# Encoder block on one core: row maxima a step earlier, a sixth score buffer, the next bias after its group, and another bank for one of the first conv units

## The chip, the cores and the metric

The kernel runs on one core of a Trainium2 chip, as one program with one launch. The metric is device time in microseconds (us) of one execution, first instruction to last; lower is better. Of the kernel before there are three timed runs and one profiled execution. The engines are called by the names that the profile uses: PE (matmuls), PEld (its weight loads), DVE (vector), ACT (activation), POOL (GpSimd), SP (which here only issues DMAs).

## The reference, cut to what matters

```python
D_MODEL = 1024; SEQ = 1024; GRID_W = 64; N_HEADS = 8; HEAD_DIM = 64

def reference(x, ...):
    u = rms_norm(x, norm1_g)
    q, k, v, cb, cc, ch, ga, gb = split(u @ w_in)
    q = rms_norm(q per head, q_norm_g); k = rms_norm(k per head, k_norm_g)
    y_a = neighbourhood_attention(q, k, v, rpb) @ w_attn_branch
    y_b = short_gated_conv(cb, cc, ch, conv_w) @ w_conv_branch
    x = x + (sigmoid(ga) * y_a + sigmoid(gb) * y_b) @ w_o
    h = rms_norm(x, norm2_g) @ w_mlp_in
    return x + square(relu(h)) @ w_mlp_out

def neighbourhood_attention(q, k, v, rpb):
    s = q k^T / sqrt(64) + bias            # 8 x 16 window on the 16 x 64 grid
    s = where(mask, s, -1e30)
    return softmax(s) @ v

def short_gated_conv(cb, cc, ch, w):       # depthwise, width 3
    z = pad(cc * ch)
    return cb * (z[:-2] * w[0] + z[1:-1] * w[1] + z[2:] * w[2])
```

Everything is float32 outside. Inside, each matmul operand is split into a high and a low half of 16 bits, and a product takes three passes (high by high, high by low, low by high).

## The kernel before

The program goes through stages on one core: the norm of x and the projections to q, k and v; a stage in which **attention and the gated conv run together**; the gates and branch products; w_o; the MLP. The change lies in the second of these, 157 to about 345 us after the span's start.

In that stage one loop (L1127) counts steps k from 0 to N + 12, with N = 64. A step stands for one *score*: head pair p = k // 16, block i of 128 queries, head e of the pair. Only the order of the instructions within the loop sets the order on each engine; every engine takes its own instructions strictly in the order in which the loop emits them, and waits on semaphores where another engine's result or buffer isn't ready.

- **Scores.** At every fourth step `at_qk(k)` (L949) emits the matmuls (L954) of four scores, k to k+3, into four score banks of PSUM, `sbank`: three with the tag "s" and one with the tag "o" (L945). A bank can be written again when the row maximum of its old score has read it.
- **Row maxima.** `at_max(s)` (L958) reads the bank on DVE, adds the bias, writes the sum to an SBUF buffer `sz` (`z`, five buffers) and leaves the row's extreme in a column of `sc`. In the trace this is the pair CUSTOM_DVE_ANT_0 and DVE_READ_ACCUMULATOR2_ANT; in the lists of instruction order it is "ISA sz,sc" and "ISA sc". Step k emits the maximum of score k-1. So the fourth maximum of a group is emitted at the step in which the next group's matmuls are emitted, just ahead of them.
- **The rest of a score.** `at_exp` on ACT (step k+1), `at_recip` on DVE, `at_hi` on ACT (the high half of P), `at_lo` on DVE (the low half, "P<-sz,sc,P"), `at_turn` (a transposing DMA from P to PT on SP's queue), `at_pv` (matmuls L1030, twelve steps after the scores) and `at_out` (qD, the attention's result, first on ACT, then on DVE).
- **The bias of the next head pair.** `bias_load` at step 3 of 16, and `bias_make` (L507: one DVE operation, "bias<-bias,sc,mk", and one on POOL, "biasm") for the two heads at steps 9 and 11.
- **Conv and gate matmuls** (L1049) fill PE between the score groups: `emit(n)` takes the next n from a generator, 9 a step at first, then 8, 6, 7, 4. A unit of 24 goes to one of three banks with the tag "d". Its reader is `conv_post` (L829): an ACT copy (L837) for the first of three kinds, DVE multiplications ("z<-ps_d,z", "cv<-ps_d,cv") for the others.
- **Weights of the next conv chunk** are split by ACT and DVE ("w_ws<-raw,sc"). `tick` moves this preparation on; `deal` gives each step up to four ticks, by a reckoning of how much DVE and ACT work was emitted in the step. At a chunk's boundary `flush` emits what is left.

The first two conv units are emitted ahead of the loop (L809), into two banks with the tag "o". There are two such banks, given out in turn, and the next two users of the tag are the fourth score bank and `hbank`, where `at_pv` writes. The copies L837 of these two units go to the conv's buffer `z`, which lies in memory that the q/k stage used until its last transposing DMA (kD<-k, L546) landed; `sz` lies there too.

Near the stage's end the scale of a gate weight (chunk S1) is worked out by `scale_s1`: its second raw tile is loaded by SP, ACT scales and squares it, DVE writes a column of `ones`, and PE sums that column over the partitions (L221, "ps_d<-ones"). `scale_of(am, more, n)` holds this matmul back until PE has been given n times 6144 more columns of work.

Of the kernel before, what the change touches and what calls it, by code (L numbers as in the profile page):

```python
# [10 lines left out]
F32 = mybir.dt.float32  # L11
# [82 lines left out]
def encoder_block(ctx: ExitStack, tc: tile.TileContext, x, weights, cols, gqk, rel, masks, out):  # L94
# [13 lines left out]
    def bank(tag):  # L108
        return psum.tile([128, 512], F32, name="ps_" + tag, tag=tag, bufs=banks[tag])
# [6 lines left out]
    def anybank():  # L116
        rc[0] += 1
        return bank("d" if solo[0] else "dsodsods"[rc[0] % 8])
# [6 lines left out]
    def cols_of(kind, n):  # L125
        a = area[kind]
        if a[1] + n > a[2]:
            assert kind != "keep"
            a[1] = a[0]
        a[1] += n  # L130
        return slice(a[1] - n, a[1])

    def keep(n=1):
        return cols_of("keep", n)

    def tmp(n=1):
        return cols_of("tmp", n)
# [64 lines left out]
    def apart(mark, n=3, of=units):  # L202
        while of[0] < mark + n and not forced[0]:
            yield WAIT
# [15 lines left out]
    def all_sum(a, out, bk, floor, lag=1):  # L220
        T.matmul(bk[:, 0:1], ones[:, 0:128], a, start=True, stop=True)  # L221
        yield
        yield from apart(units[0], lag)
        V.tensor_scalar(sc[:, out], bk[:, 0:1], floor, None, op0=OP.max)
        yield
# [145 lines left out]
    def push(*chunks):  # L371
        for ch in chunks:
            bg.append(ch.prep())
# [6 lines left out]
    for (kind, j), pieces in plan():  # L380
        ch = chunks[kind, j] = Chunk(kind, [(nk, sum(n for _, n in cs)) for _, _, nk, cs in pieces],
                                     {"A": "wa", "B": "wb"}.get(kind, "ws"), rows.get(kind, lambda j: g1)(j),
                                     j if kind == "V" else None, 9 if kind in "VQKCGS" else 0)
# [77 lines left out]
    def pow2_half(ss, top, s, inv, more=0):  # L461

        V.tensor_scalar(sci[:, ss], sci[:, ss], EXP, None, op0=OP.bitwise_and)
        yield
        V.tensor_scalar(sci[:, ss], sci[:, ss], 1.0, float(1 << 23), op0=OP.mult, op1=OP.add)
        yield
        V.tensor_scalar(sci[:, ss], sci[:, ss], 1, EXP, op0=OP.logical_shift_right, op1=OP.bitwise_and)
        yield
        V.tensor_scalar(sci[:, s], sci[:, ss], -1.0, float((190 + top) << 23), op0=OP.mult, op1=OP.add)  # L469
        V.tensor_scalar(sci[:, inv], sci[:, ss], 1.0, float((64 - top - more) << 23), op0=OP.mult, op1=OP.add)  # L470
        yield
# [30 lines left out]
    def bias_load(p):  # L502
        t = wbias.tile([128, 2, 3, 128], F32, name="bias")
        SP.dma_start(t.rearrange("p e b k -> p (e b k)"), rel[p])
        m = wbias.tile([128, 2, 384], F32, name="biasm")
        return t, m

    def bias_make(t, m, e):
        te = t[:, e].rearrange("p b k -> p (b k)")
        V.scalar_tensor_tensor(te, te, sc[:, cinv], mk[:, 0], op0=OP.mult, op1=OP.add)  # L510
        G.tensor_tensor(m[:, e], te, mk[:, 1], op=OP.add)
# [252 lines left out]
    for n, (kind, b) in enumerate(todo):  # L764
        ch = cQ if kind == "q" else cK
        if kind == "k" and b == 0:
            push(cConv[0])
        if n == 4:
# [14 lines left out]
            bias = {0: bias_load(0)}  # L783
# [22 lines left out]

    conv_start(0)
    push(cConv[1])
    first = [bank("o"), bank("o")]  # L809
    for half in range(2):  # L810
        unit(ch_mms(first[half], actU, half, cConv[0], 8, 384, 0), None, 8, 4)
        finish_qk(13 + half)
# [9 lines left out]
    w2p = p2.enter_context(tc.tile_pool(name="p2", bufs=2))  # L822
# [112 lines left out]
    N = len(steps)  # L935
    st = {}

    def rng(i):
        lo, hi = max(i - 1, 0), min(i + 1, 7)
        return lo, hi - lo + 1  # L940
# [18 lines left out]
    def at_max(s):  # L959
        p, i, e = steps[s]  # L960
        d = st[s]
        t, m = bias[p]
        if 0 < i < 7:
            bm = m[:, e]
        else:
            bm = (t[:, e, 1:3] if i == 0 else t[:, e, 0:2]).rearrange("p b k -> p (b k)")
        z = d["z"] = w2p.tile([128, 384], F32, name="sz", bufs=5)
        d["mx"] = tmp()
        V.tensor_tensor_reduce(z[:, :d["n"]], d["ps"][:, :d["n"]], bm, sc[:, cneg], 3.0e38, OP.add, OP.min,
                               accum_out=sc[:, d["mx"]])  # L970
# [36 lines left out]
    def at_pv(s):  # L1007
        p, i, _ = steps[s]
        O, PT = hbank, st[s]["PT"]
        (lo0, nb0), (lo1, nb1) = rng(i), rng(i + 1)  # L1010

        def place(u, e, sp, kb):
            lo, nb = ((lo0, nb0), (lo1, nb1))[u]
            return 12 * u + (2 * e + sp) * nb + kb - lo

        seq = [(kb, sp, sv) for kb in (i, i + 1, i - 1, i + 2) if 0 <= kb < 8 for sp, sv in PASSES]
        for n, (kb, sp, sv) in enumerate(seq):
            us = [u for u in range(2) if (lo0, lo1)[u] <= kb < ((lo0, lo1)[u] + (nb0, nb1)[u])]
            for e in range(2):
                hd = (2 * p + e) * HD  # L1020
                a = place(us[0], e, sp, kb)
                c = (i % 4 + us[0]) * 128
                if len(us) == 2:
                    b = place(1, e, sp, kb)
                    r = PT[:, a:b + 1:b - a]
                    o = O[64 * e:64 * e + 64, c:c + 256]
                else:
                    r = PT[:, a]
                    o = O[64 * e:64 * e + 64, c:c + 128]
                T.matmul(o, VT[:, kb, sv, hd:hd + HD], r, start=n == 0, stop=n == len(seq) - 1)  # L1030
        for e in range(4):
            del st[s + e]
# [25 lines left out]
    def sum_of(sm):  # L1058

        b, a = cols_of("prep", 1), ones_col()  # L1060
        V.tensor_reduce(sc[:, b], sc[:, sm], axis=AX, op=OP.add)
        V.tensor_copy(a, sc[:, b])
        return a, work[0]

    def scale_of(am, more, n=3):

        a, mark = am
        yield from apart(mark, n * 6144, work)
        b, s, inv = cols_of("prep", 1), cols_of("prep", 1), keep()
        yield from all_sum(a, b, anybank(), 1e-36)  # L1070
        yield from pow2_half(b, 14, s, inv, more)
        return s, inv

    def rows_scaled(ch, g):

        for i in range(2):
            while len(ch.raw) <= i:
                yield WAIT
            for k in range(4):
                v = ch.raw[i].rearrange("p (n k c) -> p k n c", n=2, k=4)[:, k]  # L1080
                A.activation(v, v, AF.Copy, scale=sc[:, at(g, 4 * i + k)])  # L1081
            yield

    def squares(ch, junk):

        sm = cols_of("prep", 2)
        for i in range(2):
            while len(ch.raw) <= i:
                yield WAIT
            A.activation(junk, ch.raw[i], AF.Square, accum_out=sc[:, at(sm, i)])  # L1090
            yield
        return sm

    def scale_s1():

        ch = cS[1]
        yield from rows_scaled(ch, g1)
        while len(conv_done) < 4:
            yield WAIT
        z = w2p.tile([128, S + 2], F32, name="z", bufs=1).bitcast(BF16)[:, :1024]  # L1100
        sm = yield from squares(ch, z)
        am = sum_of(sm)
        yield
        ch.s, ch.inv = yield from scale_of(am, 9, 1)

    meters = V, A = Meter(nc.vector, 0.96, 150), Meter(nc.scalar, 1.2, 190)
    debt, mark = [0.0, 0.0], [0.0, 0.0]
# [1 line left out]
    def share(k):  # L1109
        return 9 if k < 6 else 8 if k < 55 else 6 if k < 64 else 7 if k < 73 else 4  # L1110
# [16 lines left out]
    for k in range(N + 13):  # L1127
        p, w = k // 16, k % 16
        if p < 3 and w == 3:
            bias[p + 1] = bias_load(p + 1)  # L1130
        if p < 3 and w in (9, 11):
            bias_make(*bias[p + 1], (w - 9) // 2)
        ok = lambda d: 0 <= k - d < N
        early = min(4 if k % 4 else 5, share(k))
        emit(early)
        if ok(1):
            at_max(k - 1)
        if k % 4 == 0:
            if ok(0):
                at_qk(k)  # L1140
            if ok(12):
                at_pv(k - 12)
        if ok(4):
            at_hi(k - 4)
        if k % 2 and ok(3):
            at_recip(k - 3)
        if ok(5):
            at_lo(k - 5)
        if k % 2 == 0 and ok(6):
            at_turn(k - 6)  # L1150
        if ok(1):
            at_exp(k - 1)
        if 35 <= k < 59 and k % 3 == 2:
            turn_piece(1, 0, (k - 35) // 3)
        if 66 <= k < 74:
            turn_piece(2, 2, k - 66)
        if k == 60:
            bg.append(scale_s1())
        units[0] += 1
        conv_step(0)  # L1160
        if k % 4 == 2 and ok(14):
            at_out(k - 14, 0)
        if k % 4 == 3 and ok(15):
            at_out(k - 15, 1)
        deal(k)
        account(k)
        emit(share(k) - early)
# [744 lines left out]
    for n in range(28):  # L1912
        s, o = n // 7, n % 7
# [92 lines left out]
```

## Time and profile before

| what | us |
|---|---|
| timed runs: lowest, median, highest | 1224.27, 1225.31, 1226.7 |
| the profiled execution | 1225.52 |
| its span, first to last instruction | 1223.4 |
| PE busy in the span | 1192.3 (97%) |
| DVE, ACT, POOL busy | 932.5, 754.3, 450.1 |
| stage of the change, 157 to 345: PE, DVE, ACT busy of 188 | 176.84, 141.00, 130.62 |

PE's matmuls overlap each other in the list of instructions by time (a 128x512 matmul is shown with 379 ns, and its successor begins about 216 ns later), so PE's losses are read from idle time, not from durations. In square brackets such a list gives the idle time just before an instruction and what ended it. The granted clock is a share of PE's full speed.

### The profile page before, as it was taken

What the parts mean: (1) busy time and instruction counts of PE and PEld (TensorE: products, weight loads), DVE (VectorE), ACT (ScalarE), POOL (GpSimd) and SP (SyncE); (2) the same over time, 40 slices, a digit from 0 to 9 for tenths busy, and PEclk for the clock granted to TensorE, in tenths of its full rate; (3) what the DMA queues carried; (4) which work ended last, traced back from release to release, by engine and by line L of the source; (5) the groups of instructions that cost most, each with busy time, mean ns of one, the idle gap of its engine ahead of it and who ended that gap; (6) DMA issues with size and microseconds to landing.
All of it is one profiled execution on the core that took longest, in us unless ns stands there. A gap on an engine that the chain in (4) does not pass through costs nothing.

```text
span 1223.4 us, 16820 instructions
## 1 busy us (share of the span) xinstructions
PE 1192.3 (97%) x6166; PEld 570.4 (47%) x6166; DVE 932.5 (76%) x1743; ACT 754.3 (62%) x1178; POOL 450.1 (37%) x300
## 2 busy tenths in 40 slices
PE   6999999999999999999999999999999999999998
PEld 5444434444444444444458444444444444444444
DVE  7877767888668686887887665555448999998997
ACT  6756657777654454535768887787776754646440
POOL 5720012231321111101003665755647572563562
PEclk9999999999999999999999999999999999999999
DMA  7746435667551211216096654454484935335202
GB/s 256 178 165 126 104 80 111 126 118 154 113 155 37 68 56 48 69 35 259 18 179 148 207 189 143 142 189 150 135 292 163 345 128 193 152 129 199 103 35 103
DMA packets 162674, 171.24 MB, mean 140 GB/s; under 512 B 123296, under 2 KB 123808, under 8 KB 158496
## 3 DMA queue, kind: packets, MB, share of 16 engines
q1 hardware_dynamic: 162592, 170.17, 47.0%
q8 instruction: 48, 0.79, 0.3%
q14 instruction: 34, 0.28, 0.1%
HBM read 102.51 MB, written 37.75 MB: 115 GB/s over the span
## 4 chain that ended last, share of the span: by engine, by line
PE 79%; DVE 11%; ACT 3%; issue 3%; DMA 2%; POOL 1%; SPq 0%; DVEq 0%; ACTq 0%; POOLq 0%
PE ps_d L230 27%; PE ps_s L230 24%; PE ps_o L230 20%; PE ps_d L1049 4%; DVE P L89 1%; DVE sz L89 1%; PE ps_d L708 1%; DVE w_ws L89 1%; DVE sc L89 1%; DMA u2T<-v 1%; PE ps_s L708 1%; DMA raw<-in_weights 1%; ACT w_ws L89 1%; PE ps_o L1030 1%; DVE w_s L1215 1%
## 5 line engine op out<-in xcount | busy, mean ns | idle before, releaser
L230 PEld LDWEIGHTS <-ops 128*128 128x128 f16 x1356 | 132.4, 98 | 157.3
L230 PEld LDWEIGHTS <-w 128*128 128x128 f16 x1368 | 132.8, 98 | 140.7 <-DMA u2T<-v 1.3
L1049 PE MATMUL ps_d<-uT,w_ws 128*128 128x512 f16 x576 | 131.2, 386 | 0.0
L230 PE MATMUL ps_s<-ops 128*128 128x512 f16 (+1 forms) x528 | 118.3, 374 | 0.0
L230 PE MATMUL ps_d<-ops 128*128 128x512 f16 x504 | 115.6, 379 | 0.0
L230 PE MATMUL ps_d<-u2T,w 128*128 128x512 f16 (+1 forms) x504 | 110.1, 371 | 0.0
L1826 ACT ACTIVATE ops<-hf,sc 128x2048 f16<-128x2048 f32 x26 | 52.0, 1998 | 91.7 <-PE ps_d L230 54.1
L1202 POOL TENSOR_TENSOR tsum<-raw 128x512 f32<-128x512 f32 x28 | 47.3, 1703 | 141.6 <-ACT raw L1081 141.6
L1406 POOL TENSOR_TENSOR as<-as 128x512 f32<-128x512 f32 x60 | 82.5, 1376 | 41.6 <-ACT as L1686 38.0
L230 PEld LDWEIGHTS <-w_s 128*128 128x128 f16 x588 | 56.8, 98 | 69.0 <-DVE w_s L1215 0.9
L1049 PEld LDWEIGHTS <-w_ws 128*128 128x128 f16 x576 | 55.3, 99 | 67.6 <-issue 4.8
L230 PE MATMUL ps_s<-u2x,w 128*128 128x512 f16 (+1 forms) x348 | 78.6, 375 | 0.0
L1828 DVE SCALAR_TENSOR_TENSOR ops<-hf,sc,ops 128x2048 f16<-128x2048 f32 x26 | 73.0, 2808 | 4.0 <-ACT ops L1826 2.9
L1081 ACT ACTIVATE raw<-raw,sc 128x256 f32<-128x256 f32 x164 | 67.6, 494 | 11.5 <-DMA raw<-in_weights 11.5
L230 PE MATMUL ps_o<-ops 128*128 128x512 f16 x324 | 74.3, 379 | 0.0
L1202 POOL TENSOR_TENSOR gsum<-raw 128x512 f32<-128x512 f32 x14 | 18.6, 1350 | 127.1 <-ACT raw L1081 73.4
L1219 ACT ACTIVATE w<-raw,sc 128x512 f16<-128x512 f32 (+1 forms) x28 | 24.7, 928 | 52.2 <-DVE sc L469 52.2
L89 ACT ACTIVATE sz<-sz,sc 128x384 f32<-128x384 f32 (+1 forms) x64 | 37.2, 582 | 29.9 <-DVE sc L89 29.6
L1719 DVE TENSOR_TENSOR as<-ps_s,as 128x512 f32<-128x512 f32 x13 | 9.0, 692 | 57.9 <-ACT as L1738 57.9
L1842 POOL TENSOR_TENSOR raw<-raw 128x1024 f32<-128x1024 f32 x8 | 30.8, 3864 | 36.8 <-DVE ops L1836 36.8
L230 PE MATMUL ps_o<-u2T,w 128*128 128x512 f16 (+1 forms) x204 | 44.2, 366 | 0.0
L230 PEld LDWEIGHTS <-uT 128*128 128x128 f16 x288 | 28.1, 98 | 33.7
(384 smaller groups left out, 2629.8 us busy)
## 6 DMA issues: line engine op xcount, KB each, us to landing
raw<-in_weights SPq DMA_DIRECT2D x89, 512.0 KB, 5.5
hs<-as SPq DMA_DIRECT2D x16, 1792.0 KB, 8.7
hf<-hs SPq DMA_DIRECT2D x26, 1024.0 KB, 6.6
w2x<-in_weights SPq DMA_DIRECT2D x16, 512.0 KB, 7.5
raw<-in_weights SPq DMA_DIRECT2D x16, 384.0 KB, 3.6
xt<-in_x SPq DMA_DIRECT2D x8, 512.0 KB, 10.0
gs<-s SPq DMA_DIRECT2D x4, 1024.0 KB, 4.8
x<-in_x SPq DMA_DIRECT2D x8, 512.0 KB, 9.8
```

The lines of the kernel that those rows point to most:

```text
L89: return f(out, *a, **kw)
L230: T.matmul(ps, l, r, start=a, stop=b)
L708: T.matmul(vbank["q", b], UT[:, sa, k, b * 128:(b + 1) * 128], cQ.parts[:, sw, 512 * k:512 * k + 512], start=(k, n) == (0, 0), stop=(k, n) ...
L1030: T.matmul(o, VT[:, kb, sv, hd:hd + HD], r, start=n == 0, stop=n == len(seq) - 1)
L1049: T.matmul(ps, l, r, start=a, stop=b)
L1081: A.activation(v, v, AF.Copy, scale=sc[:, at(g, 4 * i + k)])
L1202: G.tensor_tensor(t[:, o], a, b, op=OP.add)
L1219: A.activation(o(0), w, AF.Copy, scale=sc[:, s])
L1406: sub.tensor_tensor(z[o], z[a], z[b], op=op)
L1826: A.activation(P[:, 1, 0], hf, AF.Copy, scale=sc[:, Rs])
L1828: V.scalar_tensor_tensor(P[:, 1, 1], hf, sc[:, Rs], P[:, 1, 0], op0=OP.mult, op1=OP.subtract)
L1842: G.tensor_tensor(w11[i2], w11[i2], w12[i2], op=OP.add)
```

## The change

Five edits, all in the attention and conv stage:

1. the second of the two first conv units goes to a "d" bank instead of an "o" bank;
2. `sz` has six buffers instead of five;
3. of a group of four scores, the first maximum stays at the step after the matmuls; the second and third come together at the next step, and the fourth a step later. The third and fourth, and with them the group's last, are thus one step sooner, and none is left at the step that emits the next group's matmuls;
4. the second `bias_make` is at step 12 of 16 instead of 11, which puts it behind the group's last maximum;
5. the factor of the S1 scale's delay is 1.4 instead of 1.

```diff
-    first = [bank("o"), bank("o")]
+    first = [bank("o"), bank("d")]
...
-        z = d["z"] = w2p.tile([128, 384], F32, name="sz", bufs=5)
+        z = d["z"] = w2p.tile([128, 384], F32, name="sz", bufs=6)
...
-        ch.s, ch.inv = yield from scale_of(am, 9, 1)
+        ch.s, ch.inv = yield from scale_of(am, 9, 1.4)
...
-        if p < 3 and w in (9, 11):
-            bias_make(*bias[p + 1], (w - 9) // 2)
         ok = lambda d: 0 <= k - d < N
         early = min(4 if k % 4 else 5, share(k))
         emit(early)
-        if ok(1):
-            at_max(k - 1)
+        for s in ((k - 1,), (k - 1, k), (k,), ())[(k - 1) % 4]:
+            if 0 <= s < N:
+                at_max(s)
         if k % 4 == 0:
             if ok(0):
                 at_qk(k)
             if ok(12):
                 at_pv(k - 12)
+        if p < 3 and w in (9, 12):
+            bias_make(*bias[p + 1], w // 12)
```

How rows move on three queues. First **ACT, at the start of the stage**, before (-) and now (+); the two L837 rows are the copies of the two first conv units:

```order
 L820 ACT_TABLE_LOAD
 L820 ACTIVATE sc<-sc 128x1
-L837 ACTIVATE z<-ps_o,sc 128x4x16x8 x2
+L837 ACTIVATE z<-ps_o,sc 128x4x16x8
+L837 ACTIVATE z<-ps_d,sc 128x4x16x8
```

The second copy now reads a "d" bank, and the fourth score bank falls on the "o" bank whose last reader was an ACT copy of the k projection, twelve ACT rows earlier.

Second, **DVE around the last maximum of scores 24 to 27** (the row "sz,sc<-ps_o"), for which the matmuls of scores 28 to 31 wait. Before:

```order
L89 SCALAR_TENSOR_TENSOR w_ws<-raw,sc,w_ws 128x384
L89 SCALAR_TENSOR_TENSOR bias<-bias,sc,mk 128x384
L89 ISA sz,sc<-ps_s,biasm,sc 128x384
L89 ISA sc 128x1
L89 RECIPROCAL sc<-sc 128x2
L89 TENSOR_SCALAR sc<-sc 128x2
L89 SCALAR_TENSOR_TENSOR P_2248<-sz,sc,P_2248 128x384
L89 SCALAR_TENSOR_TENSOR qD<-ps_o,qD 128x512
L89 SCALAR_TENSOR_TENSOR w_ws<-raw,sc,w_ws 128x384
L89 ISA sz,sc<-ps_o,biasm,sc 128x384
L89 ISA sc 128x1
```

With the change:

```order
L89 ISA sz,sc<-ps_s,biasm,sc 128x384
L89 ISA sc 128x1
L89 SCALAR_TENSOR_TENSOR P_2204<-sz,sc,P_2204 128x384
L89 SCALAR_TENSOR_TENSOR w_ws<-raw,sc,w_ws 128x384
L89 ISA sz,sc<-ps_o,biasm,sc 128x384
L89 ISA sc 128x1
L89 RECIPROCAL sc<-sc 128x2
L89 TENSOR_SCALAR sc<-sc 128x2
L89 SCALAR_TENSOR_TENSOR P_2245<-sz,sc,P_2245 128x384
L89 SCALAR_TENSOR_TENSOR qD<-ps_o,qD 128x512
L89 SCALAR_TENSOR_TENSOR bias<-bias,sc,mk 128x384
```

The last maximum has moved ahead of the reciprocal pair, of one P row and of the qD row; the bias row, which stood ahead of it, stands behind it.

Third, **SP at the end of the attention**, where the second raw tile of S1 is loaded (L253). Before:

```order
L1005 DMA_TRANSPOSE PT<-P_3258 128x12x128
L1005 DMA_TRANSPOSE PT<-P_3319 128x12x128
L1056 DMA_TRANSPOSE qD<-gs 128x4x128
L253 DMA raw<-in_weights 128x1024
L1056 DMA_TRANSPOSE qD<-gs 128x4x128
```

With the change:

```order
L1005 DMA_TRANSPOSE PT<-P_3260 128x12x128
L253 DMA raw<-in_weights 128x1024
L1005 DMA_TRANSPOSE PT<-P_3319 128x12x128
L1056 DMA_TRANSPOSE qD<-gs 128x4x128 x2
```

The load now stands ahead of one PT transpose and one qD transpose that it used to follow. On PE the sum of S1's column (L221) stands seven conv matmuls earlier than before; no other PE row changes its place, and no operation is added or removed.

## The prediction

> **What bounds the kernel now.** I read the page's busy line first, then PE's list of waits for the stage, then the list by time around each wait.
>
> ```profile
> PE 1192.3 (97%) x6166; PEld 570.4 (47%) x6166; DVE 932.5 (76%) x1743; ACT 754.3 (62%) x1178; POOL 450.1 (37%) x300
> 157.00:345.00 188.00, 176.84 (x1168) 84.35 (x1166) 141.00 (x422) 130.62 (x304) 44.21 (x58) 0.98 0.57 118
> 345.00:1223.00 878.00, 873.12 (x4251) 412.95 (x4249) 669.79 (x1015) 519.80 (x686) 355.84 (x196) 1.00 0.43 141
> PE ps_o L954 <- DVE sc L89: 7.3, 6, 2.4
> PE ps_o L954 <- ACT z L837: 2.4, 1, 2.4
> ```
>
> PE is busy 97% of the span, so a microsecond is only to be had where PE stands still or runs slowly. The two rows of windows (length, then busy PE, PEld, DVE, ACT, POOL, clock) show where: 11.16 us of idle PE in the 188 us of attention and conv, 4.88 in the 878 us after. The waits, listed one by one, are the score matmuls that wait for a bank:
>
> ```profile
> 161.09 0.32 PE L954 MATMUL ps_o<-kD,qD 64*128 64x384 f16 x1 [2.39 <-ACT z L837]
> 180.85 0.32 PE L954 MATMUL ps_o<-kD,qD 64*128 64x384 f16 x1 [0.26 <-DVE sc L89]
> 189.63 0.27 PE L954 MATMUL ps_s<-kD,qD 64*128 64x256 f16 x1 [0.53 <-DVE sc L89]
> 191.64 0.27 PE L954 MATMUL ps_o<-kD,qD 64*128 64x256 f16 x1 [1.74 <-DVE sc L89]
> 232.20 0.27 PE L954 MATMUL ps_o<-kD,qD 64*128 64x256 f16 x1 [2.43 <-DVE sc L89]
> 270.70 0.27 PE L954 MATMUL ps_o<-kD,qD 64*128 64x256 f16 x1 [1.58 <-DVE sc L89]
> 280.16 0.32 PE L954 MATMUL ps_o<-kD,qD 64*128 64x384 f16 x1 [0.42 <-DVE sc L89]
> 290.53 0.32 PE L954 MATMUL ps_o<-kD,qD 64*128 64x384 f16 x1 [0.85 <-DVE sc L89]
> 329.66 0.18 PE L221 MATMUL ps_d<-ones 128*128 128x1 bf16 x1 [0.82 <-DVE sc L89]
> ```
>
> Those put down to DVE sum to 0.26 + 0.53 + 1.74 + 2.43 + 1.58 + 0.42 + 0.85 = 7.81 us, and nearly all are for the "o" bank, a group's fourth maximum. The idle time is not all that they cost. The windows of 3.4 us behind three of them (the clock is the number before the last two):
>
> ```profile
> 162.00:165.40 3.40, 3.40 (x12) 1.24 (x10) 0.56 (x5) 0.61 (x4) 0.00 (x0) 0.55 0.00 0
> 192.60:196.10 3.50, 3.50 (x20) 1.48 (x17) 2.20 (x9) 3.50 (x11) 0.00 (x0) 0.56 0.61 116
> 232.40:235.80 3.40, 3.40 (x34) 1.92 (x31) 3.15 (x10) 2.47 (x6) 0.00 (x0) 1.00 0.67 121
> ```
>
> After the waits of 2.39 and of 0.53 + 1.74 the clock falls to about half for one stretch of that length; after the 2.43 it doesn't. Each half-speed stretch loses 3.4 x 0.5 = 1.7 us.
>
> **The change part by part.** *The bank of a first conv unit.* What releases the 2.39 us is the copy of the first conv unit out of an "o" bank:
>
> ```profile
> 158.05 0.66 PE L954 MATMUL ps_s<-kD,qD 64*128 64x256 f16 x7
> 321.68 6.22 PE L1049 MATMUL ps_d<-uT,w_ws 128*128 128x512 f16 x28
> 160.29 1.37 ACT L837 ACTIVATE z<-ps_o,sc 128x512 f32<-128x512 f32 x2 [2.55 <-DMA kD<-k]
> 160.39 0.48 DVE L89 CUSTOM_DVE_ANT_0 sz<-ps_s,bias,sc 128x256 f32<-128x256 f32 x1 [3.20 <-DMA kD<-k]
> ```
>
> The copies can't begin before the last kD transpose has landed at 160.3, and that stays. But the fourth score bank now falls on the other "o" bank, whose reader was done long before; so the wait goes, and with it the slow stretch: -2.39 - 1.7 = **-4.1**. The price: the unit in a "d" bank is read until 160.29 + 1.37 = 161.66, and the third user of the "d" banks comes after the 24 matmuls of one unit and the sum's bank, at about 163.5 when PE doesn't stop (5 of the 24 are done when the scores begin at 158.05; these are 12 matmuls, 7 of which take 0.66, so some 1.2; 19 more at 6.22 / 28 = 0.22 take 4.2). The bank is free 1.8 us ahead of that; without this cover the edit would cost what is lacking. DVE can't begin earlier than 160.39, so PE is 4.1 us further ahead of it from here on.
>
> *Maxima sooner, bias behind.* No operation is added. I work out the wait of 2.43 from DVE's rows ahead of it:
>
> ```profile
> 227.12 0.99 DVE L89 SCALAR_TENSOR_TENSOR bias<-bias,sc,mk 128x384 f32<-128x384 f32 x1
> 228.57 0.15 DVE L89 RECIPROCAL sc<-sc 128x2 f32<-128x2 f32 x1
> 228.76 0.47 DVE L89 TENSOR_SCALAR sc<-sc 128x2 f32<-128x2 f32 x1
> 229.14 1.34 DVE L89 SCALAR_TENSOR_TENSOR P<-sz,sc,P 128x384 f16<-128x384 f32 x1
> 230.41 0.68 DVE L89 SCALAR_TENSOR_TENSOR qD<-ps_o,qD 128x512 f16<-128x512 f32 x1
> 231.53 0.61 DVE L89 CUSTOM_DVE_ANT_0 sz<-ps_o,biasm,sc 128x384 f32<-128x384 f32 x1
> ```
>
> By the order of rows, the bias (0.99) and all from the reciprocal to the maximum (231.53 - 228.57 = 2.96: reciprocal, scale, P, qD and one weight split) come to stand behind it. So it ends 3.9 us sooner, at about 228.3 instead of 232.15; PE wants the bank at 232.20 - 2.43 = 229.77. The wait goes with 1.5 to spare. In the same way the waits of 1.58, 0.42, 0.85 and 0.26 each have one step's DVE rows taken from ahead of them, more than they last. For the pair 0.53 + 1.74 it is closer, as PE comes 4.1 sooner there. DVE's windows between the score groups up to it, and its longest stop:
>
> ```profile
> 161.10:171.25 10.15, 10.15 (x43) 4.10 (x43) 4.29 (x18) 4.41 (x13) 0.00 (x0) 0.83 0.01 2
> 171.25:179.77 8.52, 8.52 (x47) 3.75 (x47) 7.02 (x19) 7.05 (x17) 0.00 (x0) 1.00 0.56 150
> 179.77:188.44 8.67, 8.41 (x45) 3.56 (x45) 8.63 (x17) 4.52 (x11) 5.22 (x6) 1.00 0.30 66
> 164.73 0.16 DVE L89 TENSOR_SCALAR sc<-ps_d 128x1 f32<-128x1 f32 x1 [3.44 <-PE ps_d L221]
> ```
>
> DVE is idle 5.86 + 1.50 + 0.04 = 7.4 us, 3.44 of it behind a sum on PE that came after the stall and the slow stretch. The rows that leave the front of the maximum (a bias, P, reciprocal and scale row, and a conv row) are about 2.2. The maximum ended just ahead of 191.64; less 2.2, and less some 5 of the idle time, it ends at about 184.4, and PE wants it at 191.64 - 1.74 - 0.53 - 0.26 - 4.1 = 185.0. I take a wait of 0.4 to be safe, too short to halve the clock (-1.7).
>
> *Where the stall goes.* DVE has the same work, so the next group is late where it is tight:
>
> ```profile
> 219.97:229.01 9.04, 9.04 (x64) 4.41 (x64) 8.76 (x18) 6.48 (x16) 5.08 (x6) 1.00 0.71 123
> 229.01:240.58 11.57, 9.14 (x65) 4.42 (x64) 9.70 (x26) 7.66 (x19) 1.13 (x4) 1.00 0.63 149
> 240.58:250.11 9.53, 9.38 (x70) 4.60 (x70) 7.31 (x29) 9.53 (x28) 1.12 (x1) 1.00 0.60 99
> 268.35:279.08 10.73, 9.15 (x65) 4.41 (x64) 10.52 (x26) 6.58 (x16) 4.39 (x7) 1.00 0.56 114
> 239.91 0.17 DVE L89 RECIPROCAL sc<-sc 128x2 f32<-128x2 f32 x1 [1.38 <-ACT sz L89]
> 240.84 0.48 DVE L89 CUSTOM_DVE_ANT_0 sz<-ps_o,bias,sc 128x256 f32<-128x256 f32 x1
> ```
>
> A group takes PE some 9.1 us; DVE's share between two groups is 8.76 + 9.70 = 18.46 in the pair up to 240.58, and 10.52 in the one from 268.35. Scores 32 to 35 start at 240.58, with PE wanting the fourth bank 0.66 later. Without the 2.43 it wants it at 238.8. DVE's last maximum started 240.84 - 231.53 = 9.3 us after that of the group before, of which 1.38 was idle; behind the earlier maximum there now stand 2.96 + 0.99 = 3.9 more and one weight split more (0.6), and a reciprocal, scale and P row less (1.0). That gives 9.3 - 1.4 + 3.9 + 0.6 - 1.0 = 11.4, and 228.3 + 11.4 = 239.7: about **+0.9** comes back. By the same count scores 48 to 51 get back about 1.0, for the row of 10.52 lies 1.4 over PE's pace and a chunk's weight splits end there. Bounds for all that comes back: nothing, if ACT's results come sooner too, and 4 us, if the two tight groups lose what their predecessors gain (2.43 + 1.58). I take 2.3 with the 0.4 above, nearer the middle, since the following groups have slack (7.31 of 9.53).
>
> *Sixth buffer, S1's delay.* A score's buffer is in use a step longer; with five, the third maximum of a group would wait for a P row. The sixth costs nothing that the trace shows. The S1 sum stands seven matmuls earlier on PE (1.5 us), and it waited 0.82 already; its load stands ahead of two transposes:
>
> ```profile
> 319.56 1.56 SPq L1056 DMA_TRANSPOSE qD<-gs  x1
> 321.16 0.59 SPq L253 DMA_DIRECT2D raw<-in_weights  x1
> 325.30 1.70 ACT L89 ACTIVATE raw<-raw,sc 128x256 f32<-128x256 f32 x4 [3.29 <-DMA raw<-in_weights]
> ```
>
> Two issues of about 1.5 make 3; 0.82 + 1.5 - 3 is below nothing, so the 0.82 goes or stays in part; bounds 0 and 2.3, taken 0.6.
>
> **Sum**, against the profiled 1225.52 (span 1223.4, and 2.1 around it): 2.39 + 1.7 + 7.81 + 1.7 + 0.82 = 14.4 at the most; 2.3 + 0.6 come back; -11.5 gives 1214.0. The profiled execution lies 0.2 over the median of the runs, 1225.31, and I let that go: **1214**.
>
> [...]
>
> **The rivals.** *DVE's late start holds PE at scores 12 to 15* (a wait in the place of the removed one). If none of DVE's 7.4 us of idle time goes, the maximum ends at 191.6 - 2.2 = 189.4, PE waits from 185.0, 4.4 us, and the clock halves again. The gain is 4.1 from the bank, 7.81 - 2.27 = 5.5 from the other waits, less 4.4 - 2.27 = 2.1 that the wait grows, less 2.3 that comes back elsewhere: 5.2, so 1220.3. For it: DVE has 8.63 us of work in the 8.67 ahead. Against: the 3.44 that PE itself caused.
>
> *The clock stays.* If the slow stretches have another cause than these waits, 3.4 less is gained: 1217.4. Rows 162.00 and 192.60 each begin where a wait of over 2.2 ended, so I give it little. [...]
>
> *Only the bank pays.* DVE's work is the same, and its waits move from group to group: 1225.5 - 4.1 = 1221.4. Against: DVE is busy 141.00 of 188, and nine of the sixteen groups wait for nothing.
>
> *Slower: S1's load doesn't come along.* If its landing is bound by SP's queue or by HBM and stays at 325.30, PE reaches the sum 13.6 + 0.8 + 1.5 earlier and waits for all of it; the seven matmuls come after it and the clock halves once more: 1225.5 + 1.5 + 1.7 = 1228.7. It decides from a landing less than 3.2 us earlier. Against: the load follows PT transposes that wait for P rows, and these move with the scores.
>
> *Nothing arrives.* The stage after is fed late by its loads and takes the time back: 1225. Against: PE waits 4.88 us in 878 there.
>
> **How the numbers follow.** The forecast 0.66 (own range 1211 to 1217.5); DVE's start 0.12; the clock 0.04; only the bank 0.05; slower 0.07; nothing 0.06. Changes within 0.2% (2.45 us) can't be told from none here. Faster: 0.66 + 0.12 + 0.04 + 0.05 = 0.87; same 0.06; slower 0.07. The range runs from 1211 (nothing comes back) to 1221.5, the edge of only-the-bank.
>
> **What would show it.** Right: no wait of PE for L837; a mean clock of 1.00 from 157 to 345; PE's waits for DVE's maxima below 3 us in all, the largest at scores 32 and 48; the S1 sum waiting under 1.5. Wrong: over 2 us at scores 12 to 15, a wait of L1049 for a "d" bank, L1030 waiting for PT, or idle PE after 345 above 7 us.

## The result and the profile after

| | us |
|---|---|
| before, median of 4 runs (lowest to highest) | 1225.86 (1224.27 to 1226.7) |
| after, median of 4 runs (lowest to highest) | 1211.64 (1211.1 to 1212.64) |
| ratio, with its 95% interval | 0.9886 (0.9869 to 0.9904) |
| span of the profiled execution, before and after | 1223.4, 1209.9 |

The change makes the kernel 14.2 us faster by the medians, 13.5 by the two spans; 11.5 had been forecast. The profile of the changed kernel, first the busy line of its page, then PE's waits in the stage, then two windows (length, then busy PE, PEld, DVE, ACT, POOL, clock, DMA):

```profile
PE 1187.1 (98%) x6166; PEld 569.1 (47%) x6166; DVE 938.0 (78%) x1743; ACT 752.9 (62%) x1178; POOL 453.1 (37%) x300
```

```profile
PE ps_o L1030 <- DVE qD L89: 1.9, 4, 0.8
PE ps_o L954 <- DVE sc L89: 1.1, 1, 1.1
```

```profile
157.00:345.00 188.00, 184.98 (x1228) 89.65 (x1226) 152.07 (x436) 135.04 (x313) 48.11 (x59) 1.00 0.63 127
345.00:1209.00 864.00, 860.11 (x4190) 406.85 (x4188) 663.73 (x996) 513.58 (x676) 354.88 (x195) 1.00 0.43 141
```

In the stage PE now stands still for 188 - 184.98 = 3.0 us instead of 11.2, the clock is 1.00 throughout, and the stage after is no worse fed than before (3.9 us idle instead of 4.9). PE's wait for L837 is gone, and of the waits for row maxima one is left. A kind of wait that no step of the prediction had named stands first in the list: L1030 waits for qD rows on DVE.

PE's list by time shows both kinds, and something that the list of waits doesn't show:

```profile
157.85 0.66 PE L954 MATMUL ps_s<-kD,qD 64*128 64x256 f16 x7
158.19 0.32 PE L954 MATMUL ps_o<-kD,qD 64*128 64x384 f16 x1
...
183.29 0.77 PE L954 MATMUL ps_s<-kD,qD 64*128 64x384 f16 x7
184.06 0.27 PE L954 MATMUL ps_o<-kD,qD 64*128 64x256 f16 x1
...
219.74 0.77 PE L954 MATMUL ps_s<-kD,qD 64*128 64x384 f16 x7
220.25 0.27 PE L954 MATMUL ps_o<-kD,qD 64*128 64x256 f16 x1
...
221.09 1.01 PE L1030 MATMUL ps_o<-PT,vT 128*64 128x256 f16 x18 [0.36 <-DVE qD L89]
...
239.47 1.18 PE L1030 MATMUL ps_o<-PT,vT 128*64 128x256 f16 x24 [0.19 <-DVE qD L89]
...
265.51 0.66 PE L954 MATMUL ps_s<-kD,qD 64*128 64x256 f16 x7
267.25 0.32 PE L954 MATMUL ps_o<-kD,qD 64*128 64x384 f16 x1 [1.09 <-DVE sc L89]
...
275.95 0.82 PE L954 MATMUL ps_s<-kD,qD 64*128 64x384 f16 x7
276.72 0.32 PE L954 MATMUL ps_o<-kD,qD 64*128 64x384 f16 x1
...
277.99 1.18 PE L1030 MATMUL ps_o<-PT,vT 128*64 128x256 f16 x24 [0.62 <-DVE qD L89]
...
308.27 1.18 PE L1030 MATMUL ps_o<-PT,vT 128*64 128x256 f16 x24 [0.75 <-DVE qD L89]
315.53 1.01 PE L1030 MATMUL ps_o<-PT,vT 128*64 128x256 f16 x18
```

The distance from a group's first row to the first matmul into its "o" bank is a better gauge of a wait than the bracket. Undisturbed it is 158.19 - 157.85 = 0.34 us (narrow first block) or 220.25 - 219.74 = 0.51. At 265.51 it is 1.74, so PE lost 1.74 - 0.34 = 1.40 there, not the 1.09 in the bracket. At 183.29 it is 0.77: a loss of 0.26 without any bracket. The bracket counts idle time from the drawn end of the seven rows before, and in an undisturbed group the "o" row begins ahead of that end: by 157.85 + 0.66 - 158.19 = 0.32 us, or 219.74 + 0.77 - 220.25 = 0.26. So a bracket leaves out some 0.3. The list by time of the kernel before has such a hidden wait at the scores 32 to 35:

```profile
240.58 0.66 PE L954 MATMUL ps_s<-kD,qD 64*128 64x256 f16 x7
...
241.38 0.32 PE L954 MATMUL ps_o<-kD,qD 64*128 64x384 f16 x1
```

That is 0.80 - 0.34 = 0.46 lost. The same reckoning for every group, from both lists:

| scores from | loss before, us | listed | loss after, us | listed |
|---|---|---|---|---|
| 0 | 2.70 | 2.39 | 0 | |
| 8 | 0.58 | 0.26 | 0 | |
| 12 | 2.70 | 0.53 + 1.74 | 0.26 | none |
| 28 | 2.68 | 2.43 | 0 | |
| 32 | 0.46 | none | 0 | |
| 44 | 1.84 | 1.58 | 0 | |
| 48 | 0.74 | 0.42 | 1.40 | 1.09 |
| 52 | 1.17 | 0.85 | 0.27 | none |
| sum | 12.87 | 10.20 | 1.93 | 1.09 |

The score matmuls gain 12.87 - 1.93 = 10.9 us, the two half-speed stretches 3.4, together 14.3. From the first score matmul to the last group of L1030 the stage shrank by 12.1 (before 158.05 to 327.83, after 157.85 to 315.53), so the new waits for qD took 2.2 (1.92 in brackets). Another 1.2 was gained behind that point, 0.82 of it the S1 sum, whose wait is gone, and 0.2 ahead of the stage: 13.5, the difference of the spans.

DVE's list by time shows why the remaining waits are where they are:

```profile
183.39 0.60 DVE L89 CUSTOM_DVE_ANT_0 sz<-ps_o,biasm,sc 128x384 f32<-128x384 f32 x1
...
218.26 0.60 DVE L89 CUSTOM_DVE_ANT_0 sz<-ps_o,biasm,sc 128x384 f32<-128x384 f32 x1
...
220.36 0.68 DVE L89 SCALAR_TENSOR_TENSOR qD<-ps_o,qD 128x512 f16<-128x512 f32 x1
220.96 0.60 DVE L89 SCALAR_TENSOR_TENSOR bias<-bias,sc,mk 128x384 f32<-128x384 f32 x1
...
228.45 0.48 DVE L89 CUSTOM_DVE_ANT_0 sz<-ps_o,bias,sc 128x256 f32<-128x256 f32 x1
...
264.48 2.19 DVE L89 SCALAR_TENSOR_TENSOR w_ws<-raw,sc,w_ws 128x384 f16<-128x384 f32 x4
266.72 0.47 DVE L89 CUSTOM_DVE_ANT_0 sz<-ps_o,bias,sc 128x256 f32<-128x256 f32 x1
```

The maximum of the group 8 to 11 ends at 183.39 + 0.60 = 184.0, just when PE wants its bank. The one of the group 24 to 27 ends well before its turn; behind it come the rows that it was moved ahead of, the qD row of 220.36 among them, which ends at 221.04: PE starts L1030 at 221.09, for `hbank`, into which these matmuls write, is still being read by that row. And at 264.48 a flush of four weight splits (2.19 us) stands ahead of the last maximum of scores 44 to 47.

### The profile page after: what moved, and what is told of

It is laid out like the page before. It is cut to its first block, busy times and chain, and to the rows that moved or that the text cites. A ratio compares the mean times of both kernels' runs of the same rounds, so it can differ in the third digit from the quotient of the medians.

```text
span 1209.9 us, 16769 instructions
## 1 busy us (share of the span) xinstructions
PE 1187.1 (98%) x6166; PEld 569.1 (47%) x6166; DVE 938.0 (78%) x1743; ACT 752.9 (62%) x1178; POOL 453.1 (37%) x300
## 4 chain that ended last, share of the span: by engine, by line
PE 77%; DVE 15%; issue 3%; ACT 2%; DMA 1%; POOL 1%; SPq 0%; DVEq 0%; ACTq 0%; POOLq 0%
PE ps_d L230 27%; PE ps_s L230 23%; PE ps_o L230 19%; PE ps_d L1049 5%; DVE P L89 1%; DVE sz L89 1%; DVE w_s L1216 1%; DVE sc L89 1%; PE ps_d L708 1%; DMA raw<-in_weights 1%; DVE w_ws L89 1%; PE ps_s L708 1%; DVE sg L1339 1%; DMA u2T<-v 1%; PE ps_s L954 1%
## 5 line engine op out<-in xcount | busy, mean ns | idle before, releaser
L1049 PE MATMUL ps_d<-uT,w_ws 128*128 128x512 f16 x576 | 127.9, 379 | 0.0
L1049 PEld LDWEIGHTS <-w_ws 128*128 128x128 f16 x576 | 54.5, 98 | 65.3 <-issue 1.0
L1829 DVE SCALAR_TENSOR_TENSOR ops<-hf,sc,ops 128x2048 f16<-128x2048 f32 x26 | 76.0, 2923 | 3.6 <-ACT ops L1827 3.6
L230 PEld LDWEIGHTS <-mH 128*128 128x128 f16 x304 | 29.6, 98 | 30.4
## 6 DMA issues: line engine op xcount, KB each, us to landing
x<-in_x SPq DMA_DIRECT2D x8, 512.0 KB, 10.2
```

What stands on the lines that cost most here:

```text
L230: T.matmul(ps, l, r, start=a, stop=b)
L1049: T.matmul(ps, l, r, start=a, stop=b)
L1829: V.scalar_tensor_tensor(P[:, 1, 1], hf, sc[:, Rs], P[:, 1, 0], op0=OP.mult, op1=OP.subtract)
```

## The experiments

Each was timed beside runs of the kernel before: the first four kernels beside a median of 1224.8 (10 runs), the next four beside 1226.58 (7 runs). Ratios are to those.

**The bank alone**, in the kernel before:

```diff
-    first = [bank("o"), bank("o")]
+    first = [bank("o"), bank("d")]
```

> The kernel before with the bank edit alone. Theory: the wait for L837 (2.39 us) and the half-speed stretch behind it (1.7 us) go, and a little more, since a matmul's row runs on after the next one could have started and so hides part of a wait: 4.1 to 4.4 us less, about 1221.3. Without the sooner maxima, the waits of scores 12 to 15 (0.53 + 1.74) should stay or grow by up to 1 us, with their own half-speed stretch. Rival (DVE's late start holds PE): DVE still starts at 160.4, so what PE gains at the first scores it loses at scores 8 to 15; those waits grow by 3 to 4 us and the time stays above 1224.

Median 1221.49 us (1219.65 to 1222.64), ratio 0.997 (0.9959 to 0.9982). The wait for L837 and the slow stretch behind it are gone; the first group takes 8.82 us instead of 13.20. PE's list by time at the next places:

```profile
185.81 0.27 PE L954 MATMUL ps_s<-kD,qD 64*128 64x256 f16 x1 [0.53 <-DVE sc L89]
187.81 0.37 PE L954 MATMUL ps_o<-kD,qD 64*128 64x256 f16 x1 [1.74 <-DVE sc L89]
...
228.03 0.27 PE L954 MATMUL ps_o<-kD,qD 64*128 64x256 f16 x1 [2.43 <-DVE sc L89]
```

PE reaches the scores 12 to 15 earlier, and the waits there are 0.53 and 1.74 as before: DVE came forward with PE, so the rival in which its late start holds PE falls. What was new is that the 2.43 us, which had left the clock alone in the profile of before, has a half-speed stretch behind it here (clock 0.50 from 228.32 to 231.73), and so has the pair (from 187.36). By the medians the edit alone brings 3.3 us, less than the 4.1 to 4.4 expected, though the first group has its 4.38. A slow stretch more or less in a run, 1.7 us, is of the size of what is lacking; which of the timed runs had one is not shown.

**The maxima and the sixth buffer alone**, in the kernel before:

```diff
-        z = d["z"] = w2p.tile([128, 384], F32, name="sz", bufs=5)
+        z = d["z"] = w2p.tile([128, 384], F32, name="sz", bufs=6)
...
-        if ok(1):
-            at_max(k - 1)
+        for s in ((k - 1,), (k - 1, k), (k,), ())[(k - 1) % 4]:
+            if 0 <= s < N:
+                at_max(s)
```

> The kernel before with the sooner maxima and the sixth buffer, without the bank, the bias and the S1 edit. Theory (the terms add): the wait for L837 of 2.4 us and the slow stretch behind it stay; of the 7.81 us of waits for DVE's maxima at most 2 us are left, and 2 us come back as waits of L1030 for the qD row; no half-speed stretch at scores 12: about 7 to 8 us less, 1217.5 to 1218.5. Rival (the bias must go behind too): the two bias rows of 0.6 to 1.0 us ahead of the last maximum keep waits of over 1 us at scores 12, 28 and 44, and only 4 to 5 us are gained, about 1221.

Median 1216.63 us (1215.43 to 1217.7), ratio 0.993 (0.9918 to 0.9943). Its waits for maxima in PE's list by time are two:

```profile
189.28 0.27 PE L954 MATMUL ps_o<-kD,qD 64*128 64x256 f16 x1 [0.95 <-DVE sc L89]
...
272.25 0.32 PE L954 MATMUL ps_o<-kD,qD 64*128 64x384 f16 x1 [1.20 <-DVE sc L89]
```

This part alone brings 8.2 us of medians, the largest share and a little over the 7 to 8 expected. The maxima and the buffer were not tried apart, so no run shows whether the sixth buffer is needed. The wait for L837 is still there with its slow stretch; the wait of 2.43 is gone although the bias still stands ahead of the maximum.

**The bias back** to its place, in the changed kernel:

```diff
+        if p < 3 and w in (9, 11):
+            bias_make(*bias[p + 1], (w - 9) // 2)
...
-        if p < 3 and w in (9, 12):
-            bias_make(*bias[p + 1], w // 12)
```

> The changed kernel with the second bias at step 11 again. Theory: at scores 12 to 15 the fourth maximum ended at about 184.0 when PE wanted it, with nothing to spare, so a bias row of 0.6 to 1.0 us ahead of it makes a wait of about 1 us there; at scores 28 there are 1.4 us to spare, so none or a short one: 1 to 1.5 us more than the changed kernel, about 1212.9, and the clock stays full. Rival (the bias edit does nothing): the same as the changed kernel, 1211.6, as POOL's work on the bias comes sooner and frees DVE.

Median 1212.71 us (1212.61 to 1213.33), ratio 0.99 (0.9887 to 0.9914). One wait returns, where the bias row of step 11 stands ahead of the maximum again that the scores 12 to 15 wait for:

```profile
185.49 0.27 PE L954 MATMUL ps_o<-kD,qD 64*128 64x256 f16 x1 [0.96 <-DVE sc L89]
```

and the clock stays whole behind it. At the scores 28 there is none. So the bias edit is worth about 1.1 (against the 1211.64 of the changed kernel), at scores 12 to 15, and nothing at the place where I had counted 0.99 for it.

**S1's delay back**, in the changed kernel:

```diff
-        ch.s, ch.inv = yield from scale_of(am, 9, 1.4)
+        ch.s, ch.inv = yield from scale_of(am, 9, 1)
```

> The changed kernel with the factor 1 instead of 1.4 in the S1 scale. The sum then stands a step earlier on PE, ahead of the last L1030 group, at about 315.3. Theory: its column is ready at 313.8 since the load landed 17 us sooner, so there is no wait and the time is that of the changed kernel, 1211.6, within 0.3. Rival (the delay is what removed the wait of 0.82): PE waits 0.5 us or more for the column, and the time is 0.5 to 1.5 us longer.

Median 1211.53 us (1211.07 to 1211.97), ratio 0.9888 (0.9873 to 0.9904). The sum begins at 314.01 here, eight conv matmuls and the last L1030 group ahead of where the changed kernel has it (316.48), and waits for nothing: in the changed kernel DVE has written the column at 313.63 + 0.16 = 313.79. So the factor 1.4 only moves the sum back behind that group, where the kernel before has it too, and does nothing measurable; the wait of 0.82 went because the load came sooner.

**The changed kernel again**, beside the next three:

> The changed kernel itself, as the mark for the three beside it: 1211.6, PE's listed waits in the stage 3.0 us (1.1 of scores 48 to 51, 1.9 of L1030 for the qD row), no half-speed stretch.

Median 1211.19 us (1211.01 to 1211.66), ratio 0.9879 (0.9864 to 0.9893), with the same five waits as in the profile after, within 0.01 us.

**The bank back**, in the changed kernel:

```diff
-    first = [bank("o"), bank("d")]
+    first = [bank("o"), bank("o")]
```

> The changed kernel with both first conv units in "o" banks again. Theory: the wait of 2.4 us for L837 and one half-speed stretch come back, 4.1 to 4.4 us, and scores 12 to 15 wait for nothing: about 1215.9, which is more than the 3.3 us that the bank was worth alone, because there other waits and a slow stretch took part of it back. Rival (the two parts overlap): only the 3.3 us come back, 1214.9 or less.

Median 1215.52 us (1214.25 to 1215.67), ratio 0.991 (0.9893 to 0.9926): 4.3 more than the changed kernel beside it, the -4.1 of the prediction from the other side. PE's list by time:

```profile
161.19 0.48 PE L954 MATMUL ps_o<-kD,qD 64*128 64x384 f16 x1 [2.39 <-ACT z L837]
```

**The qD row ahead of the step's other DVE rows**, in the changed kernel, to test what L1030 waits for:

```diff
+        if k % 4 == 3 and ok(15):
+            at_out(k - 15, 1)
         if ok(4):
             at_hi(k - 4)
...
-        if k % 4 == 3 and ok(15):
-            at_out(k - 15, 1)
```

> The changed kernel with the DVE half of the qD row emitted in the same step, but ahead of the reciprocal, the weight split and the P row. Theory: the four waits of L1030 for the qD row (1.9 us in all) are an effect of the order on DVE only, and all but 0.3 us of them go; the wait of scores 48 to 51 stays at 1.1: about 1209.9. Rival (DVE is full there): the P rows come later by as much, L1030 waits for PT instead, and the time stays at 1211.6.

Median 1211.38 us (1210.59 to 1212.52), ratio 0.988 (0.9866 to 0.9895). Three of the four waits for qD are gone, so that row is what they wait for. In PE's list by time one stays, and one is new:

```profile
305.85 1.24 PE L1049 MATMUL ps_d<-uT,w_ws 128*128 128x512 f16 x5 [0.23 <-DVE cv L89]
...
307.73 1.18 PE L1030 MATMUL ps_o<-PT,vT 128*64 128x256 f16 x24 [0.65 <-DVE qD L89]
```

The time is that of the changed kernel. From the first scores to the last L1030 it is 1.1 us shorter (156.6 instead of 157.7), and the stage after has 1.0 us of listed waits where the changed kernel beside it has none.

**The same, and the maxima ahead of the step's conv emission**, against the flush at 264.48:

```diff
-        emit(early)
         for s in ((k - 1,), (k - 1, k), (k,), ())[(k - 1) % 4]:
             if 0 <= s < N:
                 at_max(s)
+        emit(early)
```

> As the one before, and each step's maxima are emitted ahead of the step's first conv matmuls, so that the weight splits that are flushed at a conv chunk's boundary stand behind the maximum of scores 47 and not ahead of it. Theory: the wait of 1.1 us goes as well, its maximum ending about 2.2 us sooner: about 1208.6. Rival: the splits are late then and the first matmuls of the chunk (L1049) wait for them, by up to 2 us: 1209.9 or more.

Median 1211.7 us (1210.27 to 1211.92), ratio 0.988 (0.9865 to 0.9895). The wait of 1.09 is gone at the scores 48, and comes up one group later in PE's list by time:

```profile
275.85 0.32 PE L954 MATMUL ps_o<-kD,qD 64*128 64x384 f16 x1 [0.98 <-DVE sc L89]
```

Its profiled span is 1208.1, 1.2 under that of the changed kernel beside it, as the stage is 1.2 us shorter (156.5 from the first scores to the last L1030); but the profiled execution is the fastest of the four (1210.27, the others 1211.65 to 1211.92), and the medians don't differ. Neither version beats the changed kernel by what can be measured, and the 1209.9 and 1208.6 expected of them failed. Why the time won in the stage is not seen in the medians stays open. In the first one's profile the waits in the stage after take it back, but such waits differ between two profiles of the changed kernel too (0.6 and none); for the second there is no profile of a run that took 1211.7.

**The clock.** The first experiment raised the question of when a wait halves the clock. The slow stretches of a run began on one grid of 3.413 us, whose phase differed from run to run: in the three profiles of before below, two stretches begin 193.05 - 162.33 = 30.72, 233.10 - 161.42 = 71.68 and 231.53 - 190.57 = 40.96 us apart, which is 9, 21 and 12 times 3.413. Read against such a grid, the profiles so far had one thing in common: a window at full speed with 1.74 us or more of idle PE, about half of it, was followed by one at half speed, and one with 1.60 or less was not. To test it, three kernels ran once more, each for one profile.

The kernel before:

> The kernel before, unchanged, for the clock. Theory: the half-speed stretches lie on a grid of 3.413 us that runs free of the program (in the runs so far its phase differs from run to run), and a stretch follows a grid window in which PE is idle for more than half, 1.71 us (so far: followed at 1.74, 1.81, 1.88, 2.17, 2.39 and 2.43 us of idle in a window, not followed at 1.60, 1.58 and less). So here the waits are the same as before (2.39; 0.53 + 1.74; 2.43; 1.58), and the stretches are those that the windows of this run's grid give: each window over 1.71 followed, none under 1.66, and the span 1223.4 with two stretches, 1.7 less with one, 1.7 more with three. Rival: the length of a wait or its place in the program decides; then the stretches are behind the 2.39 and the pair again and not behind the 2.43, wherever the grid lies.

The bank alone:

> The kernel before with the second first conv unit in a d bank, once more, for the clock. Theory: as for the kernel before run again; the waits of 0.53 + 1.74 and of 2.43 are there, and each is followed by a half-speed stretch only where over 1.71 us of it falls into one window of this run's grid; span 1219.5 with two stretches, 1217.8 with one, 1216.1 with none. Rival: place or length decides; then both are followed by a stretch again, and the span is 1219.5 within 0.5.

The kernel before, a third time:

> The kernel before a third time, for another phase of the grid. Theory and rival as for the kernel before run again: a stretch behind each window of the grid with over 1.71 us of idle PE, and behind no other; a span of 1223.4 with two stretches, 1.7 more or less for one more or less.

They took 1226.94, 1221.02 and 1224.84 us (one run each; spans 1224.8, 1218.9 and 1222.7). Windows on the grid, columns as above, idle PE being the length less the first busy number. The first profile of before:

```profile
158.92:162.33 3.41, 1.24 (x9) 0.51 (x8) 0.90 (x4) 2.04 (x5) 0.13 (x2) 1.00 0.58 147
189.64:193.05 3.41, 1.67 (x25) 1.20 (x25) 3.16 (x10) 2.61 (x7) 0.34 (x3) 1.00 0.84 192
227.18:230.60 3.42, 2.60 (x16) 0.99 (x15) 3.38 (x8) 1.22 (x3) 2.96 (x6) 1.00 0.62 115
230.60:234.01 3.41, 1.81 (x26) 1.27 (x26) 3.20 (x7) 1.77 (x5) 0.00 (x0) 1.00 0.03 5
```

The wait of 2.43 lies across an edge here, 0.82 in one window and 1.60 in the next, and the clock stayed whole behind both. The same kernel run again:

```profile
158.01:161.42 3.41, 1.56 (x12) 0.55 (x11) 0.21 (x2) 0.84 (x3) 0.13 (x2) 1.00 0.67 129
161.42:164.83 3.41, 2.87 (x10) 0.99 (x10) 0.74 (x4) 2.06 (x6) 0.00 (x0) 0.50 0.16 63
164.83:168.25 3.42, 3.42 (x11) 1.22 (x10) 1.40 (x8) 0.28 (x1) 0.00 (x0) 0.50 0.00 0
...
192.14:195.55 3.41, 1.71 (x25) 1.27 (x25) 2.92 (x9) 2.65 (x7) 0.04 (x2) 1.00 0.76 175
195.55:198.97 3.42, 3.42 (x18) 1.56 (x16) 2.32 (x9) 3.42 (x9) 0.00 (x0) 1.00 0.62 114
229.69:233.10 3.41, 0.99 (x12) 0.40 (x8) 3.41 (x7) 1.12 (x4) 0.96 (x4) 1.00 0.08 15
233.10:236.51 3.41, 3.41 (x24) 1.94 (x23) 3.17 (x10) 2.48 (x7) 0.00 (x0) 0.50 0.70 126
```

And the third time:

```profile
159.85:163.26 3.41, 1.67 (x11) 0.71 (x11) 0.90 (x4) 2.32 (x6) 0.13 (x2) 1.00 0.47 123
163.26:166.67 3.41, 3.41 (x18) 1.59 (x17) 1.56 (x9) 0.71 (x2) 0.00 (x0) 1.00 0.00 0
187.16:190.57 3.41, 1.15 (x11) 0.52 (x12) 3.38 (x12) 1.54 (x4) 0.98 (x3) 1.00 0.84 144
190.57:193.98 3.41, 3.41 (x26) 1.89 (x23) 1.98 (x8) 3.41 (x10) 0.00 (x0) 0.50 0.82 199
228.12:231.53 3.41, 0.99 (x14) 0.45 (x12) 3.41 (x7) 1.12 (x4) 0.71 (x3) 1.00 0.01 1
231.53:234.94 3.41, 3.41 (x23) 1.75 (x20) 3.01 (x9) 2.33 (x7) 0.00 (x0) 0.50 0.82 138
```

The rival falls: the same waits are followed by a slow stretch or not, as the grid lies. The 2.43 at scores 28 left the clock alone in one run of before and halved it in two; the pair at scores 12 did so in two of three; the wait for L837 in two of three. The bank alone had its two stretches again (1.95 and 2.43 us idle in their windows), which both theories had allowed. The bound that the theory gave, 1.71, is right within a few hundredths and not exact: 1.74 us of idle time was followed in the first profile and not in the third. One stretch came that it had not expected: in the second run the half-speed window from 161.42, with only 0.54 us idle, was followed by another. In the experiments half-speed windows with 0.50, 0.45 and 0.31 idle were not; more than that the runs don't show.

## Why the prediction was right, step by step

- **The bank, -4.1: right.** It measured 4.3 in the changed kernel and 4.38 in the first group of the bank alone. No matmul waited for a "d" bank there. By the medians of the bank alone it is 3.3; where the rest went is not settled.
- **The waits for maxima, 7.81: right in place, mis-sized in amount.** All of them went. What failed is that each was priced at its bracket: by the starts of the rows they cost 12.87 - 2.70 = 10.2 with the unlisted one at scores 32. The terms 2.39 and 7.81 are together 2.7 short. The reckoning from the order of rows held: at scores 28 the maximum was to end 1.5 us ahead of its turn, and it ends 1.4 ahead (218.26 + 0.60 = 218.86, against 220.25).
- **The clock, 2 x 1.7: right.** No slow stretch is left until 1208.4, 1.5 us ahead of the end. That the 2.43 had been spared in the profile of before goes with where it fell on the grid: 0.82 us in one window and 1.60 in the next.
- **Scores 12 to 15, +0.4: right.** It is 0.26; I had the maximum end at 184.4 and PE want it at 185.0, and both came at about 184.
- **Scores 32, +0.9: failed.** Nothing came back. The maxima of the two groups lie 228.45 - 218.26 = 10.2 us apart, not 11.4. I had carried durations and idle time over from rows of before. The bias row took 0.60 instead of 0.99 and the P row ahead of the qD row 1.07 instead of 1.34; two stops of 0.21 of before (at 233.49 and 237.98) are gone as well, which makes 1.1 of the 1.2. Beside the bias row POOL was busy before, and now is not:

```profile
225.97 3.24 POOL L862 TENSOR_TENSOR cv<-cv,z 128x256 f32<-128x256 f32 x4
...
216.89 3.13 POOL L862 TENSOR_TENSOR cv<-cv,z 128x256 f32<-128x256 f32 x4
```

The first row is of the kernel before and ends at 229.21, past the bias row of 227.12; the second is of the changed kernel and ends at 220.02, ahead of the one of 220.96. No run changes POOL's work alone, but the two profiles agree: the bias row took 0.99 us both times that POOL worked at L862 beside it throughout (182.82 and 227.12, both in the kernel before), and 0.60 or 0.61 in the eight cases with POOL idle. Beside the other two, both in the changed kernel, POOL was at L859: for 0.44 us and then at L862 for most of the rest (177.16, 0.85 us), and for the second half alone (257.31, 0.61 us).

- **Scores 48, +1.0: right in place**, 1.40 by the starts of rows.
- **What was missed: the qD rows, +2.2.** I had costed the moved maximum for what it stood behind, and not asked who waits for the rows that it overtook. One of these is the last reader of `hbank`, for which L1030 waits. Rows moved ahead on a busy engine are paid by the next reader behind them.
- **S1, 0.6 to come back: failed, in the safe direction.** None came back. The list by time of ACT shows the row behind the load:

```profile
308.45 1.70 ACT L89 ACTIVATE raw<-raw,sc 128x256 f32<-128x256 f32 x4 [2.16 <-DMA raw<-in_weights]
```

It was at 325.30: 16.9 us sooner, while the scores there came 13.1 sooner (306.14 to 293.02). The 3.7 beyond that is near the two DMA issues of about 3 that I had reckoned. The 1.5 set against them had nothing under it: the sum that waited has 561 matmuls L1049 and all L1030 groups of the stage ahead of it in both kernels. The one that stands seven matmuls earlier, which I took for it, is another sum of L221 (at 317.21 before, 302.59 now). And the 0.6 that I put in the place of a term below nothing had no row behind it.

- **The rivals fell, each by a run**: the late start of DVE by the bank alone, only-the-bank by the maxima alone (8.2 us), S1's load by its landing, the clock by the stretches that went with the waits. Nothing of the gain is lost in the stage after, where PE is idle for 3.9 us; the sign that would have spoken against the forecast there was 7.

So the forecast of -11.5 was 2.0 short of the spans' -13.5. The brackets hid 2.7, and S1 gave its 0.6; what came back was 1.9 + 2.2 = 4.1 instead of 2.3. That makes 2.7 + 0.6 - 1.8 = 1.5 of the 2.0; the rest lies ahead of and behind the stage. That the total came out this near is in part luck: the hidden 2.7 and the missed 2.2 of the qD rows have opposite signs. The 1211.64 lies close to the edge 1211 that stood for "nothing comes back", though 4.1 came back.

## What to carry to other kernels

Price a wait from the starts of the rows around it, against the same rows where nothing waits: the idle time in a bracket leaves out what overlapping rows cover, 0.3 us a wait here, and short waits altogether. When an instruction is moved ahead on a busy in-order engine, list what it overtakes and who waits for each of those, as carefully as what it no longer waits for. The stall of 2.43 us at the scores 28 cost another 1.7 in clock in two of three profiles of the kernel before and nothing in the third, by its place on a grid that differed from run to run, so a single profile can show a stall cheaper or dearer than it is on the average.

## What the runs showed of the hardware

In these runs the clock changed on a grid of 3.413 us whose place in the program differed from run to run: in three profiles of the kernel before its edges lay at 162.33, 161.42 and 159.85 us of the span. In this stage, behind a window at full speed with 1.81 us or more of idle PE, the next was at half speed in all eleven cases, up to 1.70 never, at 1.74 once and once not. The waits of 2.39 and 2.43 us were followed by a slow stretch in eight of ten cases. The three profiles of the kernel before had two, three and two slow stretches, worth 1.7 us each, so part of the spread between runs of the kernel before (1224.27 to 1226.7) can come from this alone: of the ten runs beside the first experiments, the three with a mean clock of 0.995, that of the profile with three stretches, took 1225.63 to 1226.27 us, and the seven with 0.997 took 1223.94 to 1225.87; the changed kernel, without such stretches, spread over 1.5 us.
